# A hybrid attention step on one core: constants of the first block in another buffer ring, attention outputs split at their source, results in the residual's buffer

## The chip, the cores and the metric

The kernel runs on 1 core of one Trainium2 chip. The metric is the device time of one execution in microseconds; the profile's times are microseconds from the start of the profiled execution. In the names below PE is TensorE, PEld its weight load, DVE VectorE, ACT ScalarE, POOL GpSimd and SP SyncE, whose queue issues nearly all DMAs.

## The reference, cut to what matters

One layer of a streaming encoder over 2048 prompt frames (16 tiles of 128 rows) and 64 sample frames with 512 cached rows:

```python
h = rmsnorm(x, g_pre)
fq, fk, fv, ff, fg, dq, dk, dv, dg = split(h @ w_in)          # 8 heads of 64, 4 heads of 2x64
fox  = softmax(fq fk^T / 8 + cum[t] - cum[s], causal) fv        # cum: running sum of log_sigmoid(ff + b)
lam  = exp(lq1.lk1) - exp(lq2.lk2) + 0.2
diff = (softmax(q1 k1^T / 8 + bias) - lam softmax(q2 k2^T / 8 + bias)) dv   # bias: table of 32 relative buckets
diff = rmsnorm(diff, subln_g) * 0.8
mixed = concat(fox * silu(fg), diff * silu(dg))
y = x + rmsnorm(mixed @ w_out, g_post)
```

Beside y the new keys, values and log-forgets are outputs. All is float32. The kernel makes each float32 product out of rounded halves: a matrix is split into a rounded part h (type fp32r) and the rest l = x - h, and a product takes three matmuls (h by h, h by l, l by h).

## The kernel before, in words

The prompt is worked off in four blocks of 512 rows. A block's input projection has eight column groups (in block 0 and 2 in the order fv, fg, fk, fq, dg, dk, dq, dv, otherwise reversed); the 64 sample rows go along in block 0 as a fifth tile. A group accumulates over eight slices k of the weights; `want_w` loads a slice (in block 0 two slices to a staging tile `wst` of ring "p", 8 buffers; later a tile `wraw` of ring "raw", 5 buffers), ACT rounds it into `wh` (L776) and DVE or POOL makes the rest `wl` (L777). The three matmuls of a slice are L872 to L874 (L869 and L870 for the sample rows). `nat_out` (L882) brings a result to a tile `ef` of ring "ef" (4 buffers). For the gate groups fg and dg `g_out` computes silu with four ACT steps (L998 to L1002) on a second tile `gw`, POOL multiplies (L1003) and SP stores to the scratch array GS (L1005).

Attention of a block runs beside the projection of the next one, and that of the last block beside the output projection of tiles 16 and 0 to 11. Its jobs are pairs of tiles (256 queries) of one of eight head pairs u (0 to 3 fox, 4 to 7 diff). A job has scores (L348, with DVE's bias add and minimum L356 and ACT's exponential L369), a second part with transposes (L487), their split (ACT `pth` L493, DVE `ptl` L494) and the product with the values (L518), and an end: `gated` transposes the gate on PE (L548), DVE multiplies it by the output into a tile `mix` (L551, ring of 1 buffer), and `store_mix` has SP store 128 KB to the scratch array MS (L386). The diagonal tile `dg` of a fox job is made by POOL (L405).

The output projection (`Out.tile`) loads a tile's mixed rows from MS as float32 (L1291), rounds them on ACT (L1292) and makes the rest on POOL (L1293). Its matmuls are L1335 to L1337. ACT brings the product to `z`, an `ef` buffer (L1351); `fin` scales z on DVE (L1376), POOL adds the residual `xres` (ring "raw") into z (L1378), and SP stores z (L1379). Tiles 12 to 15 come last, after the last attention job, with a shorter end: head pair 3's rows of MS are fetched by themselves, and SP's last DMAs store `y` (L1399).

Small constants come in `loads2`: `subl`, then `lamt` (the four lambda vectors, repeated for 128 partitions, ring "g"), `relT` (the bias table) and `cbias` (one number per head, repeated). `prologue2` computes `neglam` from lamt (DVE L1437, ACT L1440, DVE L1441 and L1442), negates cbias (DVE L1444) and builds on POOL the line of biases (31 small steps L1451, in two `ef` buffers) that goes to the scratch arrays LN and LM. The statistics of the first block end in `xv` (DVE L1127), which reads the PSUM tile `ptq`.

The order of the work is set in two steps. The program gives every piece a place on a line of nominal microseconds (`put`, `merge`; loads2 stands at 60, prologue2 at 110, an attention job's `gated` at 0.9 or 0.85 of its step); a scheduler then orders each engine's instructions by this line and by when their operands and buffers would be ready. On the chip every engine, SP's queue too, works strictly in that order.

Of the kernel before, what the change touches and what calls it, by code (L numbers as in the profile page):

```python
# [91 lines left out]
def hybrid_step(ctx: ExitStack, tc: tile.TileContext, ins, outs):  # L92
# [9 lines left out]
    def r32(ap):  # L102
        return ap.bitcast(F32)
# [35 lines left out]
    MS = [dr.tile([8, P, 256], F32, name=f"MS{b}") for b in range(SEQ // 256)]  # L139
    MN = dr.tile([8, P, DEC], F32, name="MN")  # L140
# [20 lines left out]
    class Attn:  # L161
# [222 lines left out]
        def store_mix(self, mix, u, pair, w):  # L384

            nc.sync.dma_start(out=(MN if pair is None else MS[pair])[u], in_=mix[:, :w])  # L386


        def fox(self, u, hd, pair, ctxu, first, last, sample=False):
# [54 lines left out]
            if hd == 1:  # L444
                def fin1():
                    gt = ctxu["g"][pair][0]
                    for j in range(len(tiles)):
                        for h in (0, 1):
                            c = ctxu["rc"][pair] + j
                            nc.gpsimd.tensor_scalar(out=gt[:rows, j, h * 64:(h + 1) * 64],  # L450
                                                    in0=gt[:rows, j, h * 64:(h + 1) * 64],
                                                    scalar1=ctxu["r"][:rows, h, c:c + 1], scalar2=None, op0=ALU.mult)

                def fin2():
                    c0 = ctxu["oc"][pair]
                    self.gated(ctxu["g"][pair][0], ctxu["oT"][:, c0:c0 + max(W, P)], u, pair, rows, len(tiles))
# [79 lines left out]
        def gated(self, gt, oT, u, pair, rows, nt):  # L536

            pt = ps.tile([P, BLK], F32, name="ptg", tag="pt", bufs=3)
            if pair is None:
                nc.vector.tensor_tensor(out=gt[:rows, 0, :], in0=gt[:rows, 0, :], in1=oT[:rows, :P], op=ALU.mult)  # L540
                nc.tensor.transpose(pt[:, :rows], gt[:rows, 0, :], ident[:rows, :rows])
                mix = self.p["w"].tile([P, 256], F32, name="mix", tag="mix", bufs=1)
                nc.vector.tensor_copy(mix[:, :rows], pt[:, :rows])
                self.store_mix(mix, u, pair, rows)
# [5 lines left out]
            mix = self.p["w"].tile([P, 256], F32, name="mix", tag="mix", bufs=1)  # L550
            nc.vector.tensor_tensor(out=mix[:, :W], in0=pt[:, :W], in1=oT[:, :W], op=ALU.mult)  # L551
            self.store_mix(mix, u, pair, W)
            self.G.free()

        def diff(self, u, pair, ctxu, last, sample=False):
# [92 lines left out]
            return A, B, [(0.02, fin1), (0.85, fin2)]  # L648
# [74 lines left out]
    class Proj:  # L723
# [511 lines left out]
    class Out:  # L1235
# [41 lines left out]
        def tile(self, t, late=False):  # L1277
# [11 lines left out]
            def fetch(h, l, u):  # L1289

                nc.sync.dma_start(out=r32(l), in_=src[u:u + h.shape[1], :, c0:c0 + rows].rearrange("u r t -> r u t"))  # L1291
                nc.scalar.copy(h, r32(l))  # L1292
                nc.gpsimd.tensor_tensor(out=l, in0=r32(l), in1=r32(h), op=ALU.subtract)  # L1293

            def load_last():
                fetch(*(e["m"][0, s][:, 3:4] for s in (0, 1)), 3)

            def load():
                e["m"] = {}
                if t == 16:  # L1300
# [3 lines left out]
                    fetch(e["m"][:, :, 0, :], e["m"][:, :, 1, :], 0)  # L1304
                for u in (4, 0) if t < 16 else ():
                    m = self.p["k"].tile([P, 2 * BLK], F32R, name="ml", tag="k") if late and t % 2 else \
                        self.p["e"].tile([P, 2 * BLK], F32R, name="ml", tag="er", bufs=2)
# [59 lines left out]
            def fin():  # L1367
# [5 lines left out]
                for n in (0, 1):  # L1373
# [49 lines left out]
    def loads2(g):  # L1423

        nc.sync.dma_start(out=subl, in_=subln)
        held["lam"] = g.tile([P, 2, P], F32, name="lamt", tag="g").rearrange("p a c -> p (a c)")
        nc.sync.dma_start(out=held["lam"], in_=bcast_row(lams, 256))
        held["rt"] = sm.tile([4, 32], F32, name="relT", tag="relT", bufs=1)
        nc.sync.dma_start(out=held["rt"], in_=relT)
        nc.sync.dma_start(out=cbias, in_=bass.AP(relT.tensor, relT.offset + 15, [[0, P], [32, 4]]))  # L1430

    def prologue2(e):

        lam, rt = held["lam"], held["rt"]
        ee = sm.tile([P, 4], F32, name="lame", tag="lame", bufs=1)
        for i in (0, 1):
            nc.vector.tensor_tensor_reduce(out=lam[:, 128 * i:128 * i + 64], in0=lam[:, 128 * i:128 * i + 64],  # L1437
# [6 lines left out]
        nc.vector.tensor_scalar(out=cbias, in0=cbias, scalar1=-1.0, scalar2=None, op0=ALU.mult)  # L1444
        ln = e.tile([P, BLK], F32, name="line", tag="ef")[:4]
        ln2 = e.tile([P, BLK], F32, name="line2", tag="ef")[:4]
        nc.gpsimd.memset(ln, 0.0)
        nc.gpsimd.memset(ln2, 0.0)
# [131 lines left out]
```

## Time and profile before

| | us |
|---|---|
| median of 3 runs | 1764.58 (1764.55 to 1765.37) |
| the profiled execution, whole | 1761.82 |
| its span (first to last instruction) | 1760.0 |
| PE busy in the span | 1712.5 (97%) |
| DVE, ACT, POOL busy | 1186.6, 1142.3, 693.2 |
| DMA moved | 369.93 MB, 210 GB/s |

The profile gives busy times, a chain of the work that ended last, groups of instructions by source line, and who waited for whom. In the timeline a row has start, duration, engine, line, operation, output<-inputs, shape and count; in brackets stands the idle time of the engine ahead of it and what ended that. The granted clock (PEclk) is TensorE's, as a share of full speed. Matmuls overlap, so a 128x512 matmul lasts 0.39 us in its row while the next one starts 0.227 us after it.

### The profile page before, as it was taken

What the parts mean: (1) busy time and instruction counts of PE and PEld (TensorE: products, weight loads), DVE (VectorE), ACT (ScalarE), POOL (GpSimd) and SP (SyncE); (2) the same over time, 40 slices, a digit from 0 to 9 for tenths busy, and PEclk for the clock granted to TensorE, in tenths of its full rate; (3) what the DMA queues carried; (4) which work ended last, traced back from release to release, by engine and by line L of the source; (5) the groups of instructions that cost most, each with busy time, mean ns of one, the idle gap of its engine ahead of it and who ended that gap; (6) DMA issues with size and microseconds to landing.
All of it is one profiled execution on the core that took longest, in us unless ns stands there. A gap on an engine that the chain in (4) does not pass through costs nothing.

```text
span 1760.0 us, 31267 instructions
## 1 busy us (share of the span) xinstructions
PE 1712.5 (97%) x9844; PEld 1459.2 (83%) x9844; DVE 1186.6 (67%) x3290; ACT 1142.3 (65%) x2542; POOL 693.2 (39%) x1043
## 2 busy tenths in 40 slices
PE   8999999999999999999999999999999999999998
PEld 6897988788887878888888888888878888888887
DVE  5342664556776656766777778867788777767664
ACT  4644565586776765765666668667786766566663
POOL 3331245355544543343324324443464543333331
PEclk9999999999999999999999999999999999999999
DMA  8794788889677667878767765766675465454533
GB/s 235 223 277 165 229 284 269 253 264 268 218 255 242 196 187 222 266 220 259 227 202 225 221 205 176 226 205 193 214 231 167 141 196 163 157 184 162 158 108 112
DMA packets 278404, 369.93 MB, mean 210 GB/s; under 512 B 32016, under 2 KB 167340, under 8 KB 278240
## 3 DMA queue, kind: packets, MB, share of 16 engines
q1 hardware_dynamic: 277424, 365.57, 67.8%
q0 software_dynamic: 672, 2.38, 0.4%
q8 instruction: 78, 1.28, 0.3%
q14 instruction: 86, 0.70, 0.1%
q10 hardware_dynamic: 144, 0.00, 0.0%
HBM read 263.87 MB, written 106.35 MB: 210 GB/s over the span
## 4 chain that ended last, share of the span: by engine, by line
PE 67%; DMA 13%; ACT 6%; issue 5%; DVE 5%; POOL 2%; SPq 1%; DVEq 0%; ACTq 0%; POOLq 0%
PE S L348 10%; PE pt L487 7%; PE acc L872 7%; PE acc L873 7%; PE acc L874 7%; PE av L518 5%; PE avd L518 4%; DMA wraw<-in_w_in 3%; PE acco L1335 3%; PE acco L1336 3%; PE acco L1337 3%; PE acc L1027 3%; PE acc L1028 3%; PE acc L1029 3%; DMA wst<-in_w_in 2%
## 5 line engine op out<-in xcount | busy, mean ns | idle before, releaser
L369 ACT ACTIVATE prob<-prob,mn 128x1024 f32<-128x1024 f32 (+8 forms) x400 | 356.5, 894 | 140.8 <-DVE mn L356 138.6
L348 PE MATMUL S<-kg,qg 128*128 128x512 f32 (+4 forms) x1344 | 373.9, 371 | 10.2 <-DVE mn L356 6.6
L494 DVE TENSOR_TENSOR ptl<-pt,pth 128x512 fp32r<-128x512 f32 (+3 forms) x456 | 283.7, 637 | 81.7 <-ACT pth L493 78.4
L872 PE MATMUL acc<-wh,xx 128*128 128x512 f32 x752 | 300.0, 402 | 10.8 <-ACT wh L776 5.5
L873 PE MATMUL acc<-wl,xx 128*128 128x512 f32 x752 | 298.1, 397 | 0.3
L874 PE MATMUL acc<-wh,xx 128*128 128x512 f32 x752 | 298.3, 398 | 0.0
L493 ACT CAST pth<-pt 128x512 fp32r<-128x512 f32 (+3 forms) x456 | 236.6, 545 | 79.2 <-PE pt L487 65.3
L348 PEld LDWEIGHTS S<-kg,qg 128*128 128x128 f32 (+1 forms) x1344 | 223.5, 186 | 46.9 <-DVE mn L356 14.1
L487 PE MATMUL pt<-ident,prob 128*128 128x128 f32 (+2 forms) x1692 | 254.7, 272 | 3.6 <-ACT pts L634 2.7
L487 PEld LDWEIGHTS pt<-ident,prob 128*128 128x128 f32 (+2 forms) x1692 | 199.0, 141 | 22.3 <-ACT pts L634 3.3
L777 POOL TENSOR_TENSOR wl<-wraw,wh 128x512 fp32r<-128x512 f32 x126 | 169.6, 1362 | 91.3 <-ACT wh L776 79.0
L872 PEld LDWEIGHTS acc<-wh,xx 128*128 128x128 f32 x752 | 142.4, 190 | 40.7 <-ACT wh L776 8.2
L874 PEld LDWEIGHTS acc<-wh,xx 128*128 128x128 f32 x752 | 142.5, 190 | 28.6 <-DVE xx L745 0.4
L873 PEld LDWEIGHTS acc<-wl,xx 128*128 128x128 f32 x752 | 142.8, 190 | 26.8 <-POOL wl L777 1.3
L405 POOL TENSOR_TENSOR dg<-bias,cmask 128x128 f32<-128x128 f32 (+1 forms) x136 | 66.9, 492 | 237.1 <-DVE mn L356 148.7
L518 PE MATMUL av<-pth,vg 128*128 128x256 f32 (+1 forms) x576 | 156.3, 291 | 3.2 <-ACT pth L493 2.5
L518 PE MATMUL av<-ptl,vg 128*64 128x256 f32 (+1 forms) x576 | 137.9, 280 | 1.4 <-DVE ptl L494 1.2
L776 ACT CAST wh<-wraw 128x512 fp32r<-128x512 f32 x168 | 100.2, 620 | 58.2 <-DMA wraw<-in_w_in 51.9
L518 PE MATMUL avd<-pth,vg 128*128 128x256 f32 (+1 forms) x576 | 132.3, 288 | 0.8 <-ACT pth L493 0.8
L356 DVE CUSTOM_DVE_ANT_0 prob<-S,bias,mn 128x512 f32<-128x512 f32 (+4 forms) x200 | 115.3, 576 | 15.3 <-DMA bias<-CUM 5.6
L450 POOL TENSOR_SCALAR gate<-gate,rr 128x64 f32<-128x64 f32 (+1 forms) x136 | 63.5, 477 | 150.9 <-DMA gate<-GS 75.2
L518 PEld LDWEIGHTS av<-pth,vg 128*128 128x128 f32 x576 | 108.7, 189 | 13.8 <-ACT pth L493 4.0
(262 smaller groups left out, 3537.9 us busy)
## 6 DMA issues: line engine op xcount, KB each, us to landing
wraw<-in_w_in SPq DMA_DIRECT2D x168, 256.0 KB, 5.3
vg<-VS SPq DMA_DIRECT2D x80, 512.0 KB, 5.0
qg<-QD SPq DMA_DIRECT2D x128, 256.0 KB, 4.2
kg<-KS SPq DMA_DIRECT2D x64, 512.0 KB, 4.8
wst<-in_w_in SPq DMA_DIRECT2D x64, 256.0 KB, 6.1
out<-ef SPq DMA_DIRECT2D x64, 256.0 KB, 2.5
VS<-vhl SPq DMA_DIRECT2D x32, 512.0 KB, 4.0
KS<-khl SPq DMA_DIRECT2D x32, 512.0 KB, 5.1
```

Of the source, the lines that this page charges most:

```text
L348: nc.tensor.matmul(S[:rows, :c1 - c0], q()[s][:, qc:qc + rows], kg()[ki][:, c0 - k0:c1 - k0], start=(s == 0), stop=(s == 1))
L356: nc.vector.tensor_tensor_reduce(out=pr[:rows, a - p0:b - p0], in0=S[:rows, a - c0:b - c0], in1=ap()[:rows, a - b0:b - b0], scale=1.0, sca ...
L369: nc.scalar.activation(out=pr, in_=pr, func=AF.Exp, scale=-1.0, bias=st["m"][:rows, i - 1:i], accum_out=st["s"][:rows, h:h + 1])
L487: nc.tensor.transpose(pt[:rk, off:off + rows], self.key_tile(sts[j], rows, kt, rk), ident[:rows, :rows])
L493: nc.scalar.copy(h[:rk, :off], pt[:rk, :off])
L494: nc.vector.tensor_tensor(out=l[:rk, :off], in0=pt[:rk, :off], in1=r32(h[:rk, :off]), op=ALU.subtract)
L518: nc.tensor.matmul(st["av"][:vs.stop - vs.start, j0 * rows:W], ctxu["v"][kt // 4][:rk, kt % 4, vs], g["p"][part][:rk, o:o + w], start=(kt ...
L776: nc.scalar.copy(h, raw[:, :BLK])
L777: (nc.vector if many or k % 4 == 3 else nc.gpsimd).tensor_tensor(out=l, in0=raw[:, :BLK], in1=r32(h), op=ALU.subtract)
L872: nc.tensor.matmul(a, x[0][:, c0:c0 + rows], wh, start=s, stop=False)
L873: nc.tensor.matmul(a, x[0][:, c0:c0 + rows], wl, start=False, stop=False)
L874: nc.tensor.matmul(a, x[1][:, c0:c0 + rows], wh, start=False, stop=e)
```

## The change

- Constants of block 0: lamt, relT and cbias share one tile of ring "p" (`lamt`), the bias line and all intermediates of prologue2 another (`lines`), in place of one buffer of "g", one small tile and two of "ef". loads2 moves from place 60 to 90 on the line, prologue2 from 110 to 112. POOL copies the negated cbias to its place.
- Gate intermediates of block 0: `gw` of group dg comes from ring "raw" in place of "ef" (that of fg is in "q" as before).
- Attention outputs: DVE multiplies the gate into the output's own tile (`oT` or `oTd`). A new end step `mixed` (at 0.96 or 0.94 of the job's step, `gated` of fox at 0.88) has POOL round it into `mix` and subtract into the tile, and SP store both halves (two DMAs of 128 KB in place of one; MS has a new layout with the halves side by side). `Out.tile` loads both halves ready for use: L1292 and L1293 are gone, and the load has twice the bytes.
- Results: POOL adds z and the residual into the residual's buffer xres, and SP stores from there.

```diff
+            nc.scalar.copy(mix[:, 0, :rows], pt[:, :rows])              # sample rows
+            nc.vector.tensor_tensor(out=mix[:, 1, :rows], in0=pt[:, :rows], in1=r32(mix[:, 0, :rows]), op=ALU.subtract)
...
-            mix = self.p["w"].tile([P, 256], F32, name="mix", tag="mix", bufs=1)
-            nc.vector.tensor_tensor(out=mix[:, :W], in0=pt[:, :W], in1=oT[:, :W], op=ALU.mult)
-            self.store_mix(mix, u, pair, W)
+            o = oT[:, :W]
+            nc.vector.tensor_tensor(out=o, in0=pt[:, :W], in1=o, op=ALU.mult)
             self.G.free()
+        def mixed(self, oT, u, pair, W):
...
+            mix = self.p["w"].tile([P, 256], F32R, name="mix", tag="mix", bufs=1)
+            nc.gpsimd.tensor_copy(out=mix[:, :W], in_=o)
+            nc.gpsimd.tensor_tensor(out=o.bitcast(F32R), in0=o, in1=r32(mix[:, :W]), op=ALU.subtract)
+            nc.sync.dma_start(out=MS[pair][:, u, 0, :], in_=r32(mix[:, :W]))
+            nc.sync.dma_start(out=MS[pair][:, u, 1, :], in_=o)
...
-            w = (self.p["q"].tile([P, BLK], F32, name="gw", tag="q") if b == 0 and g == "fg" else
+            w = (self.p["q" if g == "fg" else "raw"].tile([P, BLK], F32, name="gw", tag="q" if g == "fg" else "raw") if b == 0 else
...
-                nc.sync.dma_start(out=r32(l), in_=src[u:u + h.shape[1], :, c0:c0 + rows].rearrange("u r t -> r u t"))
-                nc.scalar.copy(h, r32(l))
-                nc.gpsimd.tensor_tensor(out=l, in0=r32(l), in1=r32(h), op=ALU.subtract)
+                nc.sync.dma_start(out=r32(m), in_=src[:, u:u + n, :, c0:c0 + rows].rearrange("r u s t -> r (u s) t"))
...
-                    nc.gpsimd.tensor_tensor(out=z, in0=z, in1=xr, op=ALU.add)
+                    nc.gpsimd.tensor_tensor(out=xr, in0=z, in1=xr, op=ALU.add)
...
-            line.append((60.0, len(line), lambda: loads2(pools["g"])))
-            line.append((110.0, len(line), lambda: prologue2(pe)))
+            line.append((90.0, len(line), lambda: loads2(pools["p"])))
+            line.append((112.0, len(line), lambda: prologue2(pools["p"])))
```

The scheduler's order changes with it. Three places follow; line numbers of the changed program differ from those of the program before.

DVE in the first 45 us, before: the constants stand between four weight rests and xv, the end of the block's statistics.

```order
L777 TENSOR_TENSOR wl<-wst,wh 128x512 x2
L1437 ISA lamt,lame<-lamt 128x64
L1437 ISA lame 128x1
L1437 ISA lamt,lame<-lamt 128x64
L1437 ISA lame 128x1
L1444 TENSOR_SCALAR cbias<-cbias 128x4
L1441 TENSOR_TENSOR neglam<-lame 128x1
L1442 TENSOR_SCALAR neglam<-neglam 128x1
L777 TENSOR_TENSOR wl<-wst,wh 128x512 x2
L1127 TENSOR_SCALAR xv<-ptq 128x4
```

DVE in the change, the same place (first two rows) and the place to which the constants went; the eight wl there are the slices of group fk, and L1453 and L1460 are the old L1437 and L1444.

```order
L791 TENSOR_TENSOR wl<-wst,wh 128x512 x4
L1141 TENSOR_SCALAR xv<-ptq 128x4
...
L791 TENSOR_TENSOR wl<-wst,wh 128x512 x6
L1453 ISA lines,lame<-lamt 128x64
L1453 ISA lame 128x1
L1453 ISA lines,lame<-lamt 128x64
L1453 ISA lame 128x1
L1015 SCALAR_TENSOR_TENSOR gw<-ef,gw 128x512
L1460 TENSOR_SCALAR lines<-lamt 128x4
L791 TENSOR_TENSOR wl<-wst,wh 128x512 x2
```

The constants moved from ahead of xv to between the sixth and the seventh weight rest of fk.

SP's queue, before: the constants' loads stand between the weight loads of fk (the eight) and those of fq.

```order
L773 DMA wst<-in_w_in 128x512 x8
L1425 DMA subl<-in_subln 128x1
L1427 DMA lamt<-in_lams 128x256
L1429 DMA relT<-in_relT 4x32
L1430 DMA cbias<-in_relT 128x4x1
L773 DMA wst<-in_w_in 128x512 x4
```

SP's queue in the change: they stand behind the two loads of the running sums (bias), ahead of the weight loads of dg.

```order
L1227 DMA CUM<-cum 8x512
L1239 DMA CS<-csn 8x64
L283 DMA bias<-CUM 128x512 x2
L1443 DMA lamt<-in_lams 128x256
L1444 DMA lamt<-in_relT 4x32
L1445 DMA lamt<-in_relT 128x4x1
L787 DMA wst<-in_w_in 128x512 x4
```

They moved past the first stores and loads of the block's scratch arrays.

POOL where the first attention jobs end, in the change; before, the same rows stand there without those of mix.

```order
L401 TENSOR_TENSOR dg<-bias,cmask 128x128 x2
L561 CAST mix<-oT 128x256
L562 TENSOR_TENSOR oT<-oT,mix 128x256
L446 TENSOR_SCALAR gate<-gate,rr 128x64 x2
L401 TENSOR_TENSOR dg<-bias,cmask 128x128
L561 CAST mix<-oT 128x256
L401 TENSOR_TENSOR dg<-bias,cmask 128x128
L562 TENSOR_TENSOR oT<-oT,mix 128x256
```

Two POOL steps per job came in between diagonal tiles and gates.

More of the change, by code (lines that the diff above doesn't have):

```diff
@@ L138, in hybrid_step @@
     GN = dr.tile([DEC, D], F32, name="GN")
-    MS = [dr.tile([8, P, 256], F32, name=f"MS{b}") for b in range(SEQ // 256)]
-    MN = dr.tile([8, P, DEC], F32, name="MN")
+    MS = [dr.tile([P, 8, 2, 256], F32, name=f"MS{b}") for b in range(SEQ // 256)]
+    MN = dr.tile([P, 8, 2, DEC], F32, name="MN")
     CUM = dr.tile([8, SEQ], F32, name="CUM")
@@ L456, in fin2, with fin3 @@
                     self.gated(ctxu["g"][pair][0], ctxu["oT"][:, c0:c0 + max(W, P)], u, pair, rows, len(tiles))
-                C = [(0.02, fin1), (0.9, fin2)]
+                def fin3():
+                    c0 = ctxu["oc"][pair]
+                    self.mixed(ctxu["oT"][:, c0:c0 + max(W, P)], u, pair, W)
+                C = [(0.02, fin1), (0.88, fin2), (0.96, fin3)]
             return A, B, C
@@ L541, in gated @@
                 nc.tensor.transpose(pt[:, :rows], gt[:rows, 0, :], ident[:rows, :rows])
-                mix = self.p["w"].tile([P, 256], F32, name="mix", tag="mix", bufs=1)
-                nc.vector.tensor_copy(mix[:, :rows], pt[:, :rows])
-                self.store_mix(mix, u, pair, rows)
+                mix = self.p["w"].tile([P, 2, P], F32R, name="mix", tag="mix", bufs=1)
+                nc.scalar.copy(mix[:, 0, :rows], pt[:, :rows])
+                nc.vector.tensor_tensor(out=mix[:, 1, :rows], in0=pt[:, :rows], in1=r32(mix[:, 0, :rows]),
+                                        op=ALU.subtract)
+                nc.sync.dma_start(out=MN[:, u], in_=r32(mix[:, :, :rows]))
                 self.G.free()
@@ L647, in fin2, with fin3 @@
                 self.gated(ctxu["g"][pair][0], e["o"], u, pair, rows, nt)
-            return A, B, [(0.02, fin1), (0.85, fin2)]
+            def fin3():
+                self.mixed(e["o"], u, pair, nt * rows)
+            return A, B, [(0.02, fin1), (0.85, fin2), (0.94, fin3)]
         def jobs(self, tiles, order, sample=False):
@@ L1421, in hybrid_step, with loads2, prologue2 @@
     held = {}
[L1423 removed]
+    def loads2(p):
         nc.sync.dma_start(out=subl, in_=subln)
[L1426 removed]
+        t = p.tile([P, 2 * BLK], F32, name="lamt", tag="p")
+        held["lam"], held["rt"], held["cb"] = t[:, :256], t[:4, 256:288], t[:, 288:292]
         nc.sync.dma_start(out=held["lam"], in_=bcast_row(lams, 256))
[L1428 removed]
         nc.sync.dma_start(out=held["rt"], in_=relT)
[L1430 to L1432 removed]
+        nc.sync.dma_start(out=held["cb"], in_=bass.AP(relT.tensor, relT.offset + 15, [[0, P], [32, 4]]))
+    def prologue2(p):
         lam, rt = held["lam"], held["rt"]
+        t = p.tile([P, 2 * BLK], F32, name="lines", tag="p")
         ee = sm.tile([P, 4], F32, name="lame", tag="lame", bufs=1)
         for i in (0, 1):
[L1437 removed]
+            nc.vector.tensor_tensor_reduce(out=t[:, 64 * i:64 * i + 64], in0=lam[:, 128 * i:128 * i + 64],
                                            in1=lam[:, 128 * i + 64:128 * i + 128], scale=1.0, scalar=0.0,
@@ L1442, in prologue2 @@
         nc.vector.tensor_scalar(out=neglam, in0=neglam, scalar1=LAM_INIT, scalar2=None, op0=ALU.subtract)
[L1444 to L1448, printed above, removed]
+        nc.vector.tensor_scalar(out=t[:, 128:132], in0=held["cb"], scalar1=-1.0, scalar2=None, op0=ALU.mult)
+        nc.gpsimd.tensor_copy(out=cbias, in_=t[:, 128:132])
+        ln, ln2 = t[:4, 132:388], t[:4, 388:900]
+        nc.gpsimd.memset(t[:4, 132:900], 0.0)
         for a, b, k in RUNS:
```

20 lines of the change are left out of this document (11 added, 9 removed).

## The prediction

> **What bounds the kernel now.** I read the page first, then who waited for whom on PE, then the granted clock around PE's longest waits, then the timelines there.
>
> ```profile
> span 1760.0 us, 31267 instructions
> PE 1712.5 (97%) x9844; PEld 1459.2 (83%) x9844; DVE 1186.6 (67%) x3290; ACT 1142.3 (65%) x2542; POOL 693.2 (39%) x1043
> PE 67%; DMA 13%; ACT 6%; issue 5%; DVE 5%; POOL 2%; SPq 1%; DVEq 0%; ACTq 0%; POOLq 0%
> ```
>
> PE bounds it: busy for 97%, and two thirds of the chain. The change takes no product from PE, so it can only shorten or lengthen PE's idle time, 1760.0 - 1712.5 = 47.5 us, and the stretches at half clock. The waits on PE, longest in total first, as far as the change touches them:
>
> ```profile
> PE S L348 <- DVE mn L356: 6.6, 12, 1.9
> PE acco L1335 <- ACT z L1351: 5.9, 7, 1.5
> PE acc L872 <- ACT wh L776: 5.5, 3, 3.4
> PE acc L872 <- DVE xv L1127: 3.7, 1, 3.7
> ```
>
> Columns: total us, times, longest. Two of these are single long stalls, 3.7 us and 3.4 us; the third is seven short ones in the output stage. The windows show what a long stall also costs (column before the DMA share is the granted clock):
>
> ```profile
> 44.00:48.00 4.00, 4.00 (x12) 3.09 (x12) 0.68 (x4) 3.16 (x8) 0.28 (x1) 0.57 0.90 304
> 155.00:160.00 5.00, 5.00 (x12) 3.90 (x13) 4.98 (x7) 5.00 (x11) 1.59 (x1) 0.50 0.02 9
> 1284.00:1287.00 3.00, 3.00 (x16) 3.00 (x15) 3.00 (x8) 3.00 (x8) 1.71 (x4) 0.54 0.88 264
> 1514.00:1518.00 4.00, 4.00 (x22) 3.43 (x23) 3.60 (x13) 2.62 (x6) 0.46 (x1) 1.00 0.03 10
> 1283.78 1.11 PE L487 MATMUL pt<-ident,prob 128*128 128x128 f32 x4 [2.22 <-ACT pts L634]
> 1513.22 0.73 PE L348 MATMUL S<-kg,qg 128*128 128x512 f32 x2 [1.88 <-DVE mn L356]
> ```
>
> After each of the two long stalls, and after one of 2.22 us, the clock is near 0.5 for some microseconds; after one of 1.88 us it stays at 1.00. The Trainium skill (TensorE: Matmul & The Clock Gate, Part 1) has the clock halved only after an idle window of about 3.4 us; the row with 2.22 us differs from that, and I go by the rows. By the page a stall shorter than its window would cost no clock, 1.7 us less at the lower end of term 1.
>
> **Term 1, the constants.** Before, DVE stood still for them ahead of xv:
>
> ```profile
> 31.86 1.36 SPq L1427 DMA_DIRECT2D lamt<-in_lams  x1
> 33.64 0.59 SPq L1430 DMA_DIRECT2D cbias<-in_relT  x1
> 41.80 0.17 DVE L1444 TENSOR_SCALAR cbias<-cbias 128x4 f32<-128x4 f32 x1 [2.49 <-DMA cbias<-in_relT]
> 42.18 1.29 DVE L777 TENSOR_TENSOR wl<-wst,wh 128x512 fp32r<-128x512 f32 x2
> 43.75 0.47 PE L872 MATMUL acc<-wh,xx 128*128 128x512 f32 x1 [3.68 <-DVE xv L1127]
> ```
>
> cbias was in use 8.2 us after its issue began; xv came after that, and PE waited 3.68 us for the PSUM buffer that xv reads. In the change nothing but weight rests stands ahead of xv, so this stall goes, and with it the half clock behind it: 4 us x (1 - 0.57) = 1.7 us. Gain 5.4 us. But the constants now stand on DVE between the sixth and seventh weight rest of group fk, and their loads behind bias in SP's queue:
>
> ```profile
> 73.70 0.82 SPq L283 DMA_DIRECT2D bias<-CUM  x2
> 72.44 1.07 PE L872 MATMUL acc<-wh,xx 128*128 128x512 f32 x4
> 75.20 1.28 DVE L777 TENSOR_TENSOR wl<-wst,wh 128x512 fp32r<-128x512 f32 x2
> 77.68 0.46 POOL L405 TENSOR_TENSOR dg<-bias,cmask 128x128 f32<-128x128 f32 x1 [3.13 <-DMA bias<-CUM]
> ```
>
> On the clock of before: PE starts fk at 72.44, a slice takes three starts of 0.227 us, so the seventh rest is needed at 72.44 + 6 x 0.68 + 0.23 = 76.7. DVE made the last two at 75.20, just in time. In the change bias still waits for the sums' store and is issued until 74.52; lamt, relT and cbias follow at 0.3 to 1.4 us each, cbias from 75.5 or so. It lands between 3.6 us (the second bias load, issued about 74.1 and used at 77.68) and 8.2 us (cbias itself, behind eight weight loads) later, 79.1 to 83.7; with its step of 0.17 and one rest of 0.65 the seventh rest is there at 79.9 to 84.5. PE then stands 3.2 to 7.8 us. I take 5, nearer to bias, since no row of weight loads is queued ahead of it there; plus 1.7 us of half clock. Everything shifts together when PE runs earlier, since the sums hang on PE's own transposes. ACT's exponential of lambda waits there too, with fk's roundings already behind it and PSUM buffers for several tiles free, so PE feels only the rest. POOL's 31 line steps delay two gate products of fg; the store of the first waited longer for SP's queue before, 82.82 less 79.38 us:
>
> ```profile
> 78.09 1.29 POOL L1003 TENSOR_TENSOR ef<-ef,gw 128x512 f32<-128x512 f32 x1
> 82.82 1.25 SPq L1005 DMA_DIRECT2D GS<-ef  x1
> ```
> Term 1: -5.4 + 6.7 = +1.3 us, between -0.5 and +4.1.
>
> **Term 2, the gate of dg.** Before:
>
> ```profile
> 149.07 0.53 SPq L194 DMA_DIRECT2D kg<-KS  x1
> 149.69 16.23 SPq L1005 DMA_DIRECT2D GS<-ef  x4
> 152.96 0.63 ACT L998 ACTIVATE gw<-ef 128x512 f32<-128x512 f32 x1 [8.48 <-DMA GS<-ef]
> 154.81 1.22 PE L872 MATMUL acc<-wh,xx 128*128 128x512 f32 x2 [3.39 <-ACT wh L776]
> ```
>
> Each tile of dg held two of the four ef buffers until its store landed. The store sat in SP's queue behind a key load, so ACT stood 8.48 us at the third tile's gw, with the weight roundings of dk behind it in its queue, and PE 3.39 us for those. With gw in ring "raw" a tile holds one ef buffer, and the third tile needs nothing from the store; the fifth does, at about 158 with PE's pace, after the first store has landed at 152.9. ACT's order is the same as before there. Gone: 3.39 us and half clock from 154.81 for 5.6 us, of which 155 to 160 is quoted, 2.8 us. Term 2: -6.2 us; if the last weight slice or a raw buffer comes late, nothing.
>
> **Term 3, the output stage.** ACT brought out a product into z only after an older z's store had landed:
>
> ```profile
> ACT z L1351 <- DMA out<-z: 16.6, 7, 6.1
> L1351 ACT COPY z<-acco x24: 561/586/590, 1327.2 to 1671.9; 128x512 f32<-128x512 f32 x24
> L1292 ACT CAST ml<-ml 128x512 fp32r<-128x512 f32 x29 | 18.1, 623 | 21.6 <-DMA ml<-MS 17.4 <-PE S L348 3.5 <-PE pt L487 0.6
> L1293 POOL TENSOR_TENSOR ml<-ml 128x512 fp32r<-128x512 f32 x29 | 37.4, 1292 | 38.1 <-ACT ml L1292 38.0
> ```
>
> Now z is free after POOL's addition, and the residual's buffer waits for the store; each tile needs two of ring raw's, and there are four beside the one of gpost, with some 30 us from tile to tile (12 tiles in 345 us). Of PE's 5.9 us for z I take 5 away. The roundings and rests of the loaded rows go as well: 18.1 + 37.4 us and a few of other widths, off the path (none of PE's longer waits names them). With ACT emptier by 18 us of this stage I take another 1 us. The load is twice as long; what it loses is covered by the two steps that no longer follow it. Term 3: -6 us, between 0 and -9.
>
> **Term 4, the new work on POOL.** 64 jobs, each with a rounding and a subtraction of 128x256. Nearest rows:
>
> ```profile
> L965 POOL TENSOR_TENSOR vhl<-ef,vhl 128x256 fp32r<-128x256 f32 x64 | 48.7, 781 | 57.7 <-ACT vhl L964 57.3
> 52.37 1.43 POOL L965 TENSOR_TENSOR vhl<-ef,vhl 128x256 fp32r<-128x256 f32 x2 [1.82 <-ACT vhl L964]
> L643 POOL TENSOR_SCALAR gate<-gate,ssq 128x128 f32<-128x128 f32 x64 | 40.6, 643 | 2.8
> L1113 POOL TENSOR_SCALAR rbc<-rbc 128x512 f32<-128x512 f32 x3 | 4.5, 1491 | 8.7 <-DMA rbc<-RS 8.7
> SPq L773 <- POOL wl L777: 72.3, 53, 7.5
> DMA to landing us min/median/max: 2.1/4.6/6.5
> ```
>
> The subtraction is L965's form, 0.78 us. A rounding of one input at 256 columns lies between 0.64 and 1.49, halfway by length 0.92. So 1.70 us per job, 109 us in all, against 37.4 and a few microseconds taken away in the last quarter. POOL is busy for 39%, so there is room on the average; but it works in order, and behind a mix step stand diagonal tiles, gates and weight rests, for which SP's weight loads already wait (72.3 us, the fifth row). The rounding also waits for the single mix buffer's store (landing median 4.6 us, last row), where before DVE did; DVE is rid of that. SP issues 64 more stores at about 0.4 us, 27 us of an issue queue that mostly waits. For POOL's delays I charge PE 2.5 us, between 0 and 12: at the top every tenth microsecond of the 109 reaches PE. The tail costs nothing: the last mixed rows were ready at
>
> ```profile
> 1737.40 1.43 POOL L1293 TENSOR_TENSOR ml<-ml 128x384 fp32r<-128x384 f32 x2 [1.30 <-ACT ml L1292]
> 1752.81 0.39 PE L1337 MATMUL acco<-wox,ml 128*128 128x512 f32 x1
> ```
>
> 1738.8, while PE had other tiles' products until 1752.81. There 1.70 us of POOL replace 0.3 (ACT) and 0.46 (POOL) on 128 columns, so the rows come some 1 us later; without the cover it would cost that 1 us.
>
> **The sum.** +1.3 - 6.2 - 6 + 2.5 = -8.4 us against the profiled execution's 1761.82, so 1753.4. The median of the runs, 1764.58, lies 2.8 us above that execution, so **1756.2 us**. About 0.2% (3.5 us) is what a measurement can tell from no change: faster means under 1761.1, slower over 1768.1.
>
> **Rivals.**
> (a) The constants land in time, so no stall replaces the first: chance 0.17. For it: small loads with little queued ahead; against: no load in the rows above lands faster than 3.6 us, and there are not 2 us to spare. Then term 1 is -5.4 and the time 1749.5.
> (b) The second stall stays, because dk's last weight slice or a key load keeps ACT or PE there as before: chance 0.16. For it: SP stands between 145 and 149 us for the key buffer, and the change leaves that. Against: ACT's roundings wait only for ACT itself. Then 1756.2 + 6.2 = 1762.4, no change that can be told.
> (c) Slower: POOL becomes the gate of the weight loads. 48 of the 64 jobs end beside a projection; their 48 x 1.70 = 82 us stand in POOL's queue among the 126 weight rests of ring raw's five buffers, and SP's queue holds key and query loads behind a waiting weight load. For it: SP already waits 72.3 us for those rests. Against: PE's whole wait for weights, 5.5 us, holds hardly any of that. If a quarter of the 82 us reaches PE, 20 us, the time is 1756.2 - 2.5 + 20 = 1773.7. It decides the sign once about (8.4 + 2.5 + 3.5) / 82 = 18% of it reaches PE. Chance 0.14. The Trainium skill (SBUF — State Buffer, on the shared port pair) says that VectorE with two SBUF inputs and GpSimd lock each other out for a whole instruction, which speaks for (c); here the same POOL step of 128x256 takes 1.43 / 2 = 0.71 us in a quiet stretch and 0.78 on the mean, so a lock shows only as a tenth.
>
> The forecast has 0.53; its own range is 1750 to 1761. The range with 8 in 10: down to (a) with the lower end of term 3, 1749.5 - 3 = 1746; up past (b) with POOL's share doubled, 1767. Faster: 0.51 of the forecast, (a), and a little of (b): 0.71. Same: the rest of (b) and the forecast's upper edge: 0.16. Slower: 0.13.
>
> **What would show it.** Right: no PE wait for xv near 40 us, but one near 71 us for a weight rest, behind DVE's wait for a constant, with the clock at 0.5 after it; no wait of 3 us near 150 us and no wait of ACT for a GS store there; PE's waits for z under 1 us; POOL busy about 755 us (693 + 109 - 43). Wrong: PE idle as large as 47 us again; waits for weights of more than 10 us, with POOL named in SP's waits for much more than 72 us; the last rows' products ending PE's queue late in the tail.

## The result, and the profile after

The changed program took 1776.95 us (median of 4 runs, 1776.54 to 1781.35), beside 1764.57 us for the program before: a ratio of 1.0067, with a 95% interval of 1.0046 to 1.0088. It is 12.4 us slower, where 8.4 us faster was forecast, and it lies above the stated range. Its profiled execution took 1776.64 us.

The page and the waits on PE of the changed program (us in total, times, longest):

```profile
span 1774.8 us, 31496 instructions
PE 1714.6 (97%) x9844; PEld 1457.5 (82%) x9844; DVE 1204.7 (68%) x3290; ACT 1125.9 (63%) x2513; POOL 722.7 (41%) x1134
```

```profile
PE S L348 <- DVE mn L356: 13.5, 21, 1.6
PE acco L1349 <- DMA ml<-MS: 6.0, 4, 1.8
PE ptk L991 <- ACT ef L896: 5.8, 1, 5.8
...
PE acc L887 <- DVE wl L791: 2.6, 2, 2.4
...
PE acco L1349 <- ACT z L1365: 0.7, 1, 0.7
```

PE's idle time is 1774.8 - 1714.6 = 60.2 us, where it was 47.5. Of the waits that the prediction named, xv near 40 us, wh near 150 us and most of z (0.7 us for 5.9) are gone. New are one of 2.4 us for a weight rest, one of 5.8 us, 6.0 us for rows from memory, and twice the wait for scores.

To see where the time arises, I compare two profiled executions at equal amounts of PE's work: each matmul counts with the lower quartile of the start-to-start times of its shape in the program before (1542 us in all), and at a given sum the start of one is taken from that of the other. Changed minus before, in us:

| PE's work done | 40 | 80 | 120 | 200 | 1160 | all |
|---|---|---|---|---|---|---|
| start of that matmul, before | 53 | 94 | 135 | 226 | 1312 | 1753 |
| changed program | -3.1 | +1.1 | +9.3 | +3.1 | +7.0 | +14.8 |

So block 0 goes down, up twice and down again; attention between 200 and 1160 loses a little, and the output stage loses 7.8 us. Single executions vary: one kernel below whose instructions between the marks 200 and 1160 are those of the program before (d_res) goes from -0.5 to +4.1 us there, so a few microseconds there tell nothing, and the medians of the runs below decide.

The first new stall is the forecast one. SP, DVE and PE of the changed program:

```profile
73.31 0.42 SPq L1443 DMA_DIRECT2D lamt<-in_lams  x1
78.26 0.22 DVE L1453 CUSTOM_DVE_ANT_0 lines<-lamt 128x64 f32<-128x64 f32 x1 [7.18 <-DMA lamt<-in_lams]
79.99 0.50 PE L887 MATMUL acc<-wl,xx 128*128 128x512 f32 x1 [2.35 <-DVE wl L791]
```

DVE stood 7.18 us for lamt, which was in use 5 us after its issue began; PE stood 2.35 us for the weight rest behind it. The second was not forecast. POOL, SP, ACT and PE 20 us later, with the windows (granted clock ahead of the DMA share):

```profile
97.15 2.09 POOL L1476 DMA_DIRECT2D LM<-LN  x4 [4.66 <-DMA LN<-lines]
...
100.80 2.62 SPq L1088 DMA_DIRECT2D xn<-in_xp  x1
103.51 1.49 SPq L1004 DMA_DIRECT2D KS<-khl  x1
105.09 7.11 SPq L1088 DMA_DIRECT2D xn<-in_xp  x3
...
112.59 0.58 ACT L997 CAST khl<-ptk 128x512 fp32r<-128x512 f32 x1 [10.11 <-DMA KS<-khl]
...
113.85 0.69 PE L991 MATMUL ptk<-ident,ef 64*128 64x64 f32 x4 [5.82 <-ACT ef L896]
```

```profile
104.00:108.00 4.00, 4.00 (x30) 3.82 (x29) 0.00 (x0) 0.00 (x0) 0.00 (x0) 1.00 1.06 299
108.00:112.00 4.00, 0.02 (x1) 0.00 (x0) 0.00 (x0) 0.00 (x0) 0.00 (x0) 1.00 1.06 325
112.00:116.00 4.00, 2.15 (x11) 2.04 (x12) 1.02 (x2) 2.67 (x6) 0.00 (x0) 0.52 1.08 394
116.00:118.00 2.00, 2.00 (x11) 2.00 (x11) 1.72 (x5) 1.45 (x4) 0.00 (x0) 0.50 1.02 411
```

The four expansions of the bias line (575.5 KB each) are issued at 97 us. From 104 to 118 us the DMA engines are full; SP needs 7.11 us to issue three row loads that took 2.73 us in the program before; a key store lands so late that ACT waits 10.11 us for its buffer, and PE 5.82 us for ACT; then the clock is 0.5 for some microseconds. SP, too, has a new wait just ahead of this: 4.3 us at a weight load, until the store of the line to LN has landed, since the tile `lines` now holds a buffer of ring "p". In the program before, whose three row loads stand first here, POOL issued the expansions at 131 us, since the line's two buffers of ring ef kept its steps behind the statistics of block 1:

```profile
101.25 2.73 SPq L1074 DMA_DIRECT2D xn<-in_xp  x3
113.00 0.20 POOL L155 TENSOR_TENSOR rt<-xrs 128x8 f32<-128x8 f32 x1 [30.30 <-DVE qhl L1052]
...
115.14 8.40 POOL L1451 TENSOR_SCALAR line<-line,relT 4x38 f32<-4x38 f32 x31
...
131.13 2.09 POOL L1461 DMA_DIRECT2D LM<-LN  x4 [4.34 <-DMA LN<-line]
```

In the output stage SP has a wait that was not there. SP's waits of the changed program that matter here, and its queue after one tile:

```profile
SPq L787 <- POOL wl L791: 59.9, 45, 7.8
...
SPq L563 <- POOL mix L561: 21.5, 16, 10.6
...
SPq L1300 <- DMA out<-xres: 20.2, 20, 2.8
...
SPq L564 <- POOL oT L562: 14.8, 12, 3.1
```

```profile
1421.21 0.42 SPq L1394 DMA_DIRECT2D out<-xres  x1
1422.26 0.34 SPq L1300 DMA_DIRECT2D xres<-in_xp  x1
1422.70 0.53 SPq L271 DMA_DIRECT2D qg<-QD  x1
...
1426.44 0.33 SPq L1300 DMA_DIRECT2D xres<-in_xp  x1
1426.86 3.10 SPq L1305 DMA_DIRECT2D ml<-MS  x2
```

The residual's load for a later tile stands in SP's queue right behind the stores of the residual's buffers, or a few rows later, so SP waits until the store that frees its buffer has landed, with queries and rows behind it.

### The profile page after: what moved, and what is told of

The parts are those of the page before. It is cut to its first block, busy times and chain, and to the rows that moved or that the text cites. A ratio compares the mean times of both kernels' runs of the same rounds, so it can differ in the third digit from the quotient of the medians.

```text
span 1774.8 us, 31496 instructions
## 1 busy us (share of the span) xinstructions
PE 1714.6 (97%) x9844; PEld 1457.5 (82%) x9844; DVE 1204.7 (68%) x3290; ACT 1125.9 (63%) x2513; POOL 722.7 (41%) x1134
## 4 chain that ended last, share of the span: by engine, by line
PE 64%; DMA 14%; DVE 9%; ACT 5%; issue 5%; POOL 2%; SPq 1%; DVEq 0%; ACTq 0%; POOLq 0%
PE S L348 9%; PE pt L486 7%; PE acc L886 7%; PE acc L887 7%; PE acc L888 6%; PE av L517 6%; PE avd L517 3%; DVE prob L356 3%; PE acco L1349 3%; PE acco L1350 3%; PE acco L1351 3%; DMA wraw<-in_w_in 3%; PE acc L1041 2%; PE acc L1042 2%; PE acc L1043 2%
```

## The experiments

All times are medians of 5 to 11 runs beside runs of the program before on the same chip; those had medians of 1764.28, 1763.06, 1764.74 and 1762.85 us in the four sets.

**The four parts, each alone in the program before.** a_const has only the constants' edit, b_gate only the line of gw, c_split the attention outputs and the loads of rows (MS, mixed, fetch), d_res only the result's tile.

> The program before with only the constants of block 0 moved (one tile of ring p for their loads, another for the bias line and intermediates, places 90 and 112). Theory A, that the line expansions LM<-LN now run at 97 to 112 us into the key stores and residual-row loads: the stall of 3.7 us at 40 us is gone (-5.4), one of about 2.4 us is at 77 us (+4.2), one of about 5.8 us at 108 us (+8.1), and the stall for dg's weights at 151 us stays in whole or in part (0 to -6.2 of it absorbed, since PE arrives later): 1765 to 1774 us. Rival, that the loss at 108 us came with the gate or with the split: no wait over 2 us between 100 and 115 us, 1762 to 1766 us.

> The program before with only the gate intermediates of dg in ring raw. If the prediction's second term was right by itself: no wait of PE over 2 us near 150 us, 6.2 us less, 1758 us. Rival, that the stall went only because the constants made everything there later: the wait stays or moves, 1763 to 1765 us.

> The program before with only the attention outputs split where they arise (and loaded ready for use); the results stay in z. Theory S, that the split makes the output stage longer (64 stores and twice the loaded bytes in SP's queue, POOL's steps late, PE waiting for ml from DMA): 6 to 12 us slower, 1771 to 1777 us, with PE's wait for ml<-MS at 4 us or more. Rival R, that the residual's buffer does it: 1760 to 1766 us, and PE waits for z as before.

> The program before with only the results added into the residual's buffer and stored from there. Rival R: SP stands for the stores of the residual's buffers (about 20 us in all) ahead of later loads, so rows and keys come late: 5 to 10 us slower, 1770 to 1775 us. Theory S: the waits for z go and nothing else comes, 3 to 6 us faster, 1759 to 1762 us.

| run | median, us | less before | ratio | interval |
|---|---|---|---|---|
| a_const | 1765.86 | +1.6 | 1.0008 | 0.9989 to 1.0028 |
| b_gate | 1759.80 | -4.5 | 0.9981 | 0.9963 to 0.9999 |
| c_split | 1773.81 | +9.5 | 1.0044 | 1.0025 to 1.0064 |
| d_res | 1771.85 | +7.6 | 1.0044 | 1.0025 to 1.0064 |

I had put theories S and R against each other as the one cause in the output stage; both the split and the residual's buffer cost time, so neither alone holds. In c_split PE waited 2.1 us for `ml<-MS`, where theory S looked for 4 or more, so the way that it gave for the split's cost isn't seen. The gate gains by itself. The constants come out at nothing, but not for the reason forecast: the two waits on PE in the trace of a_const, and the comparison at equal work (-4.5 us at 40, +0.4 at 80, +8.2 at 120, +1.1 at 200), show a second stall, and that the gate's stall of the program before is swallowed behind it.

```profile
PE ptk L977 <- ACT ef L882: 5.7, 1, 5.7
...
PE acc L873 <- DVE wl L777: 3.0, 1, 3.0
```

**Block 0: the expansions, and the constants' places.** ab is a_const with the gate. ab_lines is ab with

```diff
-        ln, ln2 = t[:4, 132:388], t[:4, 388:900]
-        nc.gpsimd.memset(t[:4, 132:900], 0.0)
+        ln = pe.tile([P, BLK], F32, name="line", tag="ef")[:4]
+        ln2 = pe.tile([P, BLK], F32, name="line2", tag="ef")[:4]
+        nc.gpsimd.memset(ln, 0.0)
+        nc.gpsimd.memset(ln2, 0.0)
```

and ab_fix is ab with

```diff
-            line.append((90.0, len(line), lambda: loads2(pools["p"])))
-            line.append((112.0, len(line), lambda: prologue2(pools["p"])))
+            line.append((60.0, len(line), lambda: loads2(pools["p"])))
+            line.append((150.0, len(line), lambda: prologue2(pools["p"])))
```

> The constants and the gate of dg together, as in the change, and nothing else of it. If the four parts add up (constants +1.6, gate -4.5): 1761.4 us, with the stalls at 77 us (2.4 to 3 us) and 108 us (5.7 us) and none at 151 us. Rival, that the late PE already swallows the gate's stall, so that the gate gains nothing beside the constants: 1765 to 1767 us.

> The run ab, but with the bias line's two tiles back in ring ef, so that POOL computes them, stores them and issues the expansions LM<-LN after the statistics of block 1, at 125 to 135 us as in the program before; the constants stay where the change put them. Theory A, that the expansions among the key stores make the stall at 108 us: no wait over 2 us between 100 and 115 us, the one at 77 us stays, 8 us less than the run ab: 1753 to 1757 us. Rival, that the stall comes from the order of the row loads and key stores in SP's queue, whatever else moves bytes then: the wait of 5.7 us stays, 1761 to 1766 us.

> The run ab, with the constants loaded at place 60 as before and their use at place 150. No part of the constants should then stand ahead of a weight rest that PE waits for: no stall at 40, 77, 108 or 151 us, so 5.4 + 6.2 = 11.6 us less than before: 1753 us. Rival, that block 0 is held by something else once those stalls are gone (the weight loads, DMA at its full share from 100 us on): 1757 to 1761 us, with other waits of PE of 2 us or more before 200 us.

| run | median, us | less before | ratio | interval | at work 120 | at 200 |
|---|---|---|---|---|---|---|
| ab | 1765.26 | +2.2 | 1.0019 | 1.0003 to 1.0036 | +6.9 | +0.7 |
| ab_lines | 1756.67 | -6.4 | 0.9966 | 0.9942 to 0.9990 | -2.1 | -9.2 |
| ab_fix | 1751.16 | -11.9 | 0.9937 | 0.9921 to 0.9954 | -4.3 | -11.4 |

Beside the constants the gate gains nothing (ab against a_const): its rival was right. With the line's two tiles back in ring ef the expansions are issued at 136 us, the wait near 108 us is gone, and 8.6 us with it. The edit also takes away SP's wait for the line's store (4.5 us in ab) and moves the 31 line steps, so it doesn't part these from the expansions. Full DMA engines alone aren't the cause: from 100 to 112 us their share is 1.08 in ab_lines too, with PE busy throughout, and around the late expansions they are as full, but then PE has no key store to wait for. The waits of PE up to 180 us in ab_lines, and the windows around its expansions:

```profile
PE acc L872 <- ACT xx L744: 1.8, 2, 1.4
PE acc L873 <- DVE wl L777: 1.6, 1, 1.6
```

```profile
136.00:140.00 4.00, 4.00 (x19) 3.34 (x18) 0.02 (x1) 3.00 (x5) 3.39 (x5) 1.00 1.02 273
140.00:144.00 4.00, 4.00 (x19) 3.30 (x19) 0.69 (x1) 3.18 (x7) 1.29 (x1) 1.00 0.99 357
```

ab_fix, with the constants loaded early and used late, has none of the four stalls, and is the fastest version here, 11.9 us under the program before; 11.6 was expected.

**The split: POOL's steps.** c_nopool is c_split without the two POOL steps, c_touch has a step on one column in their place, c_round only the rounding, c_dummy two steps on a scratch tile, c_gq the two stores in POOL's queue (nc.gpsimd.dma_start).

```diff
-            mix = self.p["w"].tile([P, 256], F32R, name="mix", tag="mix", bufs=1)
-            nc.gpsimd.tensor_copy(out=mix[:, :W], in_=o)
-            nc.gpsimd.tensor_tensor(out=o.bitcast(F32R), in0=o, in1=r32(mix[:, :W]), op=ALU.subtract)
-            nc.sync.dma_start(out=MS[pair][:, u, 0, :], in_=r32(mix[:, :W]))
+            nc.gpsimd.tensor_scalar(out=o[:, :1], in0=o[:, :1], scalar1=1.0, scalar2=None, op0=ALU.mult)
+            nc.sync.dma_start(out=MS[pair][:, u, 0, :], in_=o)
             nc.sync.dma_start(out=MS[pair][:, u, 1, :], in_=o)
```

(c_touch; c_nopool has no tensor_scalar, c_round keeps the tile, its copy and its store), and c_dummy:

```diff
             nc.sync.dma_start(out=MS[pair][:, u, 0, :], in_=o)
             nc.sync.dma_start(out=MS[pair][:, u, 1, :], in_=o)
+            mix = self.p["w"].tile([P, 256], F32, name="mix", tag="mix", bufs=1)
+            nc.gpsimd.memset(mix, 0.0)
+            nc.gpsimd.tensor_tensor(out=mix, in0=mix, in1=mix, op=ALU.subtract)
```

> The run c_split without POOL's rounding and subtraction: both stores of an attention output send the output itself, unsplit, right behind DVE's product (the split of the attention outputs is left out). Theory P, that POOL's lateness is what the split costs (SP stands behind mix and the output's rest, POOL's queue delays diagonal tiles and gates): most of the 9.5 us goes, 1763 to 1767 us. Theory D, that the doubled stores and the doubled loads of rows cost it: 1770 to 1775 us.

> The run c_split with POOL's two steps of each job (0.40 and 0.74 us) replaced by one step on a single column of the output at the same place in POOL's queue; both stores send the unsplit output (the split is left out). Theory W, that the cost is the place in the queue (POOL stands for DVE's gated product, 86 us in the changed program, with diagonal tiles, gates and weight rests behind it): the loss stays, 1770 to 1776 us. Theory B, that the cost is POOL's busy time of 1.14 us a job: as without the steps, 1758 to 1762 us.

> The run c_split with the two stores of each job issued from POOL's own queue behind the subtraction, in place of SP's. Theory Q, that the cost of POOL's lateness is passed on by SP, which stands for mix and for the output's rest (36 us in the changed program) with loads behind: 1760 to 1767 us. Theory B or W (POOL's own queue is what delays): 1772 us or more, since the issues come on top of POOL's work.

> The run c_split without POOL's subtraction (the lower half is stored unsplit): POOL rounds, 0.40 us a job, so 26 of 73 us of its new work are left. Busy time as the cost: 1761.5 + 12 x 26/73 = 1766 us. If the lateness or the single mix tile costs it, which are left as they were: 1770 us or more.

> The run c_nopool with POOL given a fill and a subtraction of 128x256 per job on a scratch tile that no other step reads, about 1.1 us a job as in c_split (the split is left out). Busy time as the cost: 1770 to 1775 us, as c_split. Lateness of the stores and hold of the output tiles as the cost: 1759 to 1763 us, as c_nopool.

| run | POOL busy, us | median, us | less before | ratio | interval |
|---|---|---|---|---|---|
| c_nopool | 644.5 | 1759.84 | -3.2 | 0.9980 | 0.9963 to 0.9998 |
| c_touch | 667.9 | 1761.53 | -3.2 | 0.9996 | 0.9974 to 1.0017 |
| c_round | 678.4 | 1771.04 | +8.2 | 1.0053 | 1.0031 to 1.0076 |
| c_dummy | 716.9 | 1779.91 | +17.1 | 1.0088 | 1.0062 to 1.0114 |
| c_split | 725.8 | 1773.81 | +9.5 | 1.0044 | 1.0025 to 1.0064 |
| c_gq | 795.5 | 1795.75 | +31.0 | 1.0194 | 1.0165 to 1.0223 |

c_nopool and c_touch have the doubled stores and loads, c_touch also the place in POOL's queue, and lose nothing: theories D and W fall. c_dummy's stores leave at once and nothing reads its scratch tile, yet by its median it is slower than c_split, and slower than either expectation: lateness of the stores isn't needed either. The cost isn't in proportion to POOL's time. Over the six runs the time rises by 34 us for 151 us more of POOL, 0.23 us for each microsecond, but 21 us of that come with c_gq alone. c_round takes 8.2 us with a third of the work; its theory of proportion (1766 us) lies a little below its interval (1.0031 of 1762.85 is 1768.3), and the other one, lateness or the single mix tile (1770 us or more), was met, though c_dummy is slow without either. The profiled executions say the same: behind the mark 200 of PE's work they lose, against the program before, 0.8 us in c_nopool and 1.4 in c_touch, but 10.2 in c_round, 8.6 in c_split and 8.2 in c_dummy (whose profiled execution is the fastest of its seven), and 35.7 in c_gq. So what costs is shown to be POOL's whole steps of each job, and how the cost grows with them is not. c_gq doesn't decide between SP and POOL, since the issues add 70 us to POOL. The rows of POOL in c_split give the true prices:

```profile
L562 POOL TENSOR_TENSOR oT<-oT,mix 128x256 fp32r<-128x256 f32 x32 | 25.6, 799 | 1.1
L562 POOL TENSOR_TENSOR oTd<-oTd,mix 128x256 fp32r<-128x256 f32 x32 | 25.0, 782 | 1.8
L561 POOL CAST mix<-oTd 128x256 fp32r<-128x256 f32 x32 | 13.6, 426 | 56.5 <-DVE oTd L552 44.7 <-DVE oss L1383 6.9 <-DVE cc L598 3.3
L561 POOL CAST mix<-oT 128x256 fp32r<-128x256 f32 x32 | 13.2, 412 | 57.5 <-DVE oT L552 41.0 <-issue 7.2 <-DMA MS<-mix 5.2
```

They sum to 77.4 us, 1.2 us a job. By which wait this reaches PE stays open: no one row of PE's waits holds it (the largest, for scores behind DVE's mn, is 11.3 us in c_split, 10.2 in c_nopool). Each kernel is ordered anew by the scheduler on all engines, and no run held that order fixed, so a part of the cost may be the order.

**The split on other engines.** best1 is ab_fix with the split, rounding on ACT and subtraction on DVE:

```diff
-            nc.gpsimd.tensor_copy(out=mix[:, :W], in_=o)
-            nc.gpsimd.tensor_tensor(out=o.bitcast(F32R), in0=o, in1=r32(mix[:, :W]), op=ALU.subtract)
+            nc.scalar.copy(out=mix[:, :W], in_=o)
+            nc.vector.tensor_tensor(out=o.bitcast(F32R), in0=o, in1=r32(mix[:, :W]), op=ALU.subtract)
```

> The run ab_fix with the attention outputs split where they arise, but the rounding on ACT and the subtraction on DVE, so that POOL has no step of them; results stay in z. If the gains of ab_fix (11.9 us) and of the split without POOL's steps (3.2 us) add up: 1748 us. If ACT's and DVE's new steps (64 of about 0.4 us each) delay scores: 1751 to 1758 us.

1768.03 us, ratio 1.0023 (1.0005 to 1.0041): both expectations were too low. At equal work it is 13.2 us ahead of the program before at 200, 0.4 ahead at 1000, 0.6 behind at 1160 and 3.7 behind at the end, so it lost its gain beside the attention jobs. SP waited 37.4 us for ACT's rounding in it. Against ab_fix it loses 15 us, more than the split with its steps on POOL lost against the program before: the steps aren't free on ACT and DVE either. Which of the two engines costs the time wasn't tried.

**The results: which buffer is held.** d_res_gq is d_res with the residual's loads in POOL's queue. In d_free neither z nor xres is held by a store; it leaves the results out and stores a copied column and the constant:

```diff
                     nc.gpsimd.tensor_tensor(out=xr, in0=z, in1=xr, op=ALU.add)
+                    nc.gpsimd.tensor_copy(out=one, in_=xr[:, 511:512])
+                    nc.sync.dma_start(out=yo[:, 511:512], in_=one)
+                    nc.sync.dma_start(out=yo[:, :511], in_=self.gp[n][:rows, :511])
```

In d_hold both are held:

```diff
+                    nc.gpsimd.tensor_tensor(out=z[:, :256], in0=z[:, :256], in1=xr[:, :256], op=ALU.add)
+                    nc.gpsimd.tensor_tensor(out=xr[:, 256:], in0=z[:, 256:], in1=xr[:, 256:], op=ALU.add)
+                    nc.sync.dma_start(out=yo[:, :256], in_=z[:, :256])
+                    nc.sync.dma_start(out=yo[:, 256:], in_=xr[:, 256:])
```

> The run d_res with the residual's loads (of the tiles that aren't last) issued from POOL's queue in place of SP's. Theory R, that SP stands 34.5 us for the stores of the residual's buffers (22 waits) with rows, keys and bias behind it: that wait leaves SP, and the 7.6 us go: 1760 to 1766 us. Rival, that the order on DVE and ACT (the scaling of z and its wait for POOL's statistics ahead of scores) costs it: 1770 to 1775 us.

> The run d_res, but what is stored of the result is one column of it, copied by POOL to a small tile, and for the rest the constant gpost (the results are left out), so that neither z nor the residual's buffer waits for a store to land, and SP still waits for POOL. Theory R, that holding the residual's buffer until its store lands costs the time: 1758 to 1764 us. Rival Z, that the early release of z and the order that follows from it cost it: 1769 to 1774 us.

> The program before with POOL's sum put half into z and half into the residual's buffer, each stored from there, so that z is held until its store lands as before, and the residual's buffer as in d_res. Theory R: as slow as d_res or slower, 1770 to 1776 us. Rival Z: as the program before, 1763 to 1766 us.

| run | median, us | less before | ratio | interval | SP waits for out<-xres, us (times) |
|---|---|---|---|---|---|
| d_res | 1771.85 | +7.6 | 1.0044 | 1.0025 to 1.0064 | 34.5 (22) |
| d_hold | 1767.96 | +5.1 | 1.0025 | 1.0008 to 1.0043 | 17.6 (13) |
| d_res_gq | 1769.08 | +4.3 | 1.0033 | 1.0015 to 1.0050 | 5.8 (4) |
| d_free | 1758.98 | -3.9 | 0.9972 | 0.9951 to 0.9993 | none |

With z early and no buffer held the edit gains 3.9 us; with the residual's buffer held it loses, and the less SP waits for it the less. So the loss goes with that hold (theory R), and the early z isn't its cause: rival Z falls. One rival stands untested: the four kernels differ in the order of all engines in the output stage, which the scheduler makes anew. d_hold lies between what the two theories expected, with half of d_res's wait. d_res_gq came out between its two expectations: POOL now issues most of the loads and waits 23.0 us in SP's stead (its busy time is 710.5 us for 693.2); the loads of the last tiles stay with SP. At equal work the output stage behind the mark 1160 loses 10.8 us in d_res (whose profiled execution is the slowest of its ten), 6.9 in d_hold, 1.0 in d_res_gq and nothing in d_free; d_res_gq lost its other 7 us ahead of that mark. The wait in d_res, and SP's queue after a tile, where the first of two loads stands until 1486.04 behind stores issued by 1481.15:

```profile
SPq L1286 <- DMA out<-xres: 34.5, 22, 4.8
```

```profile
1479.57 1.58 SPq L1380 DMA_DIRECT2D out<-xres  x2
1486.04 1.00 SPq L1286 DMA_DIRECT2D xres<-in_xp  x2
1487.14 0.38 SPq L1291 DMA_DIRECT2D ml<-MS  x1
```

How SP's wait reaches PE stays open. DVE's waits for bias tiles in the output stage (1300 us to the end) grew, as these rows of d_res and then of the program before show:

```profile
DVE prob L356 <- DMA bias<-CUM: 12.8, 8, 2.5
```

```profile
DVE prob L356 <- DMA bias<-CUM: 6.5, 5, 2.2
```

Scores wait for those tiles, and PE's wait for scores behind them (S <- mn) was 3.8 us there before and 7.5 in d_res. But in d_free, which gains, DVE waits nearly as long, and PE's wait for scores is 1.7 us:

```profile
DVE prob L356 <- DMA bias<-CUM: 10.4, 4, 3.5
```

In d_hold, which loses, PE's wait for scores is 2.4 us. So bias tiles and scores can be at most a part of it.

## Why the prediction was wrong

- **Term 1, the constants: right as a sum, incomplete in its mechanism.** +1.3 us was forecast, +1.6 measured. The stall for xv went (-4.5 us at work 40; 5.4 forecast), and the forecast stall behind the constants came, with 2.35 us in place of 5: lamt was in use 5 us after its issue began, nearer to bias than I took it, and below my lower bound of 3.2. What the step left out is that POOL's line steps also carry four expansions of 575.5 KB, which were priced nowhere once the line's buffers no longer held them back. With the line in ring p they and SP's wait for the line's store cost 8.6 us (ab against ab_lines). In a_const that is hidden by the next point, so the agreement of the sum is luck.
- **Term 2, the gate of dg: right alone, nothing in company.** -6.2 us forecast, -4.5 measured (-7.1 at work 200). With the constants beside it the same stall was already covered by the later PE, so it gained nothing there (+2.2 us with it, +1.6 without). I had added the two terms as if they were apart. The two together were forecast at -4.9 and gave +2.2.
- **Term 3, the output stage: the step that failed by its sign.** -6 us was forecast. The waits for z went from 5.9 to 0.7 us in the whole (3.6 are left in d_res). "the residual's buffer waits for the store; each tile needs two of ring raw's, and there are four" counted when the buffer is needed, and not where its load stands: close behind the store in SP's queue, so that all behind it waits for the landing (34.5 us of SP in d_res). The edit alone cost 7.6 us. The gain is real where no buffer is held (d_free, -3.9). The removal of L1292 and L1293 gained 3.2 us together with the doubled stores and loads (c_nopool); in c_touch the interval allows for nothing.
- **Term 4, POOL: price too high, share too low.** 1.70 us a job was forecast, 1.2 measured (rounding 0.42, not 0.92); POOL's busy time came to 722.7 us, not 755 (the prediction's own terms, 693 + 109 - 43, make 759). But c_split less c_nopool is 12.7 us by the medians (11.3 by the ratios), not 2.5: some 15% of the 77 us. That is the upper end of the bound, and the kind of rival (c): POOL's steps count, but not by its mechanism, since SP's wait for POOL's weight rests didn't grow (72.3 us before, 59.9 after). The 39% of busy time was no cover.
- **Half clock.** Terms 1 and 2 charge 1.7 and 2.8 us of half clock with their stalls. That fits here (4.2 us for the stall of 2.35 us at 79.99, and -6.3 for the gate's in b_gate), but it doesn't always come: in c_split PE paused 2.93 us at the gate's place, and the clock stayed at 1.00.
- **Sum.** The four parts alone give 1.6 - 4.5 + 9.5 + 7.6 = +14.2 us, and the whole +12.4; from ab on it is 2.2 + 9.5 + 7.6 = +19.3. They don't add exactly; in the whole SP's wait for out<-xres is 20.2 us and not 34.5.
- **Rivals.** (a) and (b) concern block 0. The constants didn't land in time; no wait of 2 us remained near 150 us. (c) had 0.14 and a price of 20 us; slower had 0.13 in all.

## What to carry to other kernels

A buffer that a store must leave before the next load may fill it can cost time not when the buffer is needed but where that load stands in the in-order queue: look at the rows close behind the store. A step moved off a full path carries its DMAs with it, and taking away the buffer that held it back lets them collide with others, as the expansions did at 97 us; stalls that lie close together don't add up, since a later PE covers the next one. And with PE at 97%, whole steps on an engine that is 39% busy still cost 11 to 20 us here against the run without them, for 27 to 77 us of work: measure a dummy step before counting it as hidden.

## What the runs showed of the hardware

DVE and POOL block each other where both subtract SBUF tiles. Two stretches of the changed program; in each POOL makes two weight rests (1.27 us each in the second, undisturbed) and DVE one (about 0.68 us where nothing disturbs it, like the qhl at 856.29):

```profile
282.14 3.00 POOL L791 TENSOR_TENSOR wl<-wraw,wh 128x512 fp32r<-128x512 f32 x2
282.27 1.72 DVE L791 TENSOR_TENSOR wl<-wraw,wh 128x512 fp32r<-128x512 f32 x1 [0.34 <-ACT wh L790]
...
853.00 2.55 POOL L791 TENSOR_TENSOR wl<-wraw,wh 128x512 fp32r<-128x512 f32 x2 [0.41 <-ACT wh L790]
854.96 1.14 DVE L791 TENSOR_TENSOR wl<-wraw,wh 128x512 fp32r<-128x512 f32 x1
856.29 0.68 DVE L1066 TENSOR_TENSOR qhl<-qf,qhl 128x512 fp32r<-128x512 f32 x1
```

At 854.96 DVE waits until POOL's second ends at 855.55 and takes 0.55 us from there. At 282.27 it starts behind POOL's first and POOL's second behind it, so POOL's pair takes 3.00 us. The prediction looked for this in POOL's rows alone, found a tenth, and thought the lock of the Trainium skill (SBUF — State Buffer, Who interferes with whom) small; DVE's rows show it whole, as that section has it. It hardly explains the split's cost: the DVE weight rests of this group take 903 ns on the mean in c_nopool and 917 in c_split, and DVE as a whole is busy for 1190.0 and 1196.1 us.

The clock fell to half after PE's pause of 2.35 us at 79.99 us too, as the window of the changed program shows:

```profile
82.00:84.00 2.00, 2.00 (x6) 1.59 (x5) 0.00 (x0) 1.87 (x3) 2.00 (x10) 0.50 0.99 159
```

It did so after 2.22 us in the program before. The length of the pause alone doesn't decide it, though. In ab_lines the clock fell after 1.92 us (first two rows), and in d_res it stayed at 1.00 after 3.14 us (last two):

```profile
1275.77 1.11 PE L487 MATMUL pt<-ident,prob 128*128 128x128 f32 x4 [1.92 <-ACT pts L634]
1277.00:1279.00 2.00, 2.00 (x10) 2.00 (x10) 2.00 (x5) 2.00 (x5) 0.81 (x2) 0.50 0.87 284
1638.84 0.62 PE L348 MATMUL S<-kg,qg 128*128 128x384 f32 x2 [3.14 <-DVE mn L356]
1640.00:1642.00 2.00, 2.00 (x11) 1.66 (x10) 1.80 (x5) 0.00 (x0) 0.33 (x1) 1.00 0.66 187
```

What does decide it stays open. The idle window of about 3.4 us that the Trainium skill gives (TensorE: Matmul & The Clock Gate, Part 1) is not needed here.
